# Inverting triangular blocks by a substitution of 32x32 instead of 16x16 blocks on GpSimd, without one level of small matmuls, and with unread products in the lead-in

## The chip, the cores and the metric

One core of a Trainium2 chip runs the whole layer in one launch. The time is the device's own, in microseconds, and the median of several executions counts. The engines are named as in the profile: PE is TensorE (products), PEld its weight loads, DVE is VectorE, ACT is ScalarE, POOL is GpSimd, and SP is SyncE, which only issues DMA transfers here.

## What is computed

The reference is a hybrid decoder layer in float32 for 512 tokens with 16 meta tokens ahead of them, width 1024, 16 heads of 64 channels. After a first layer norm one wide product (`w_in`) makes the inputs of two branches: attention in a sliding window of 128 tokens, and a recurrent mixer (RWKV-7). Both are gated per channel and added, projected (`w_out`), normalised with the residual, and sent through an MLP with a squared ReLU (1024 to 4096 to 1024) and a last norm. The mixer is where the change lies. For each head it keeps a 64x64 state S:

```
def step(S, inp):
    r_t, w_t, k_t, v_t, kk_t, a_t = inp
    sa = jnp.einsum('bhij,bhj->bhi', S, -kk_t)
    S = S * w_t[:, :, None, :] + sa[..., None] * (kk_t * a_t)[:, :, None, :] + v_t[..., None] * k_t[:, :, None, :]
    return S, jnp.einsum('bhij,bhj->bhi', S, r_t)
```

Taken in chunks of 64 tokens, the dependence of each step on the earlier ones within its chunk is a unit triangular system of 64x64 per chunk and head, N, and the kernel needs the inverse of that triangle.

## The kernel before

**Precision and the dense stream.** A float32 product of a weight tile with activations is made as three products of high and low parts: high by high, low by high, high by low (`three`, L476 to L478). ScalarE casts the high part of a weight tile (`whi`, L628), VectorE subtracts to get the low part (`wlo`, L630). These dense products run through the whole first two thirds of the kernel, since `w_in` has 52 tiles of 512 KB, and the mixer's and the attention's own products are woven between them. The MLP's products come at the end (L1560 to L1562 and L476 to L478 with `dps`).

**What sets the order.** Every operation is recorded by `op(engine, cost, fn, r=..., w=..., new=...)` with what it reads and writes. `ORDER`, a list of 2804 numbers written into the file, then says in which order the recorded operations are issued, and `SLOTS` which buffer of a ring each new tile gets. Each engine works through its own operations strictly in that order, and an operation waits for semaphores when what it reads or overwrites isn't done. So an operation that stands too early on an engine holds up all behind it.

**The lead-in.** x comes in four blocks of 128 tokens. Per block VectorE makes the statistics (L732, L735 to L737), GpSimd the power -0.5 (L740), and then ScalarE normalises blocks 0 and 1 (L752), VectorE blocks 2 and 3 (L755). TensorE transposes 16 tiles of blocks 0 and 1, the meta tokens' eight small ones (L764), and 16 tiles of blocks 2 and 3 (L787); the evictions (L797 on VectorE, L793 on ScalarE) put a scale and a bias on and split them into `hhi` and `hlo` (L802). Ahead of it TensorE transposes a table of per-channel rows (L710), which comes by DMA. Then the dense products begin.

**One pair of heads in the mixer.** Heads are taken two at a time (`rwkv`, pairs j = 0 to 7), with 8 chunks of 64 tokens. In `NT` lie the negated triangles N transposed, two heads above each other on 128 partitions. Per pair:

- the scores (L1000, 16 products of 128x128) give N and the matrices `GR`; VectorE masks them into `NT` (L1008) and `GR`;
- SyncE writes N to a scratch in DRAM (`Nd`, L1023 and L1025), and reads it back (L1077) so that each of the 64 diagonal 16x16 blocks, and two of the meta tokens, lies on one of 66 partitions of `Nf`;
- GpSimd inverts all 66 blocks at once by substitution. Step s multiplies the columns found so far with row s of N (L1092) and adds that on (L1096), 15 steps of two instructions;
- SyncE writes the result to DRAM (`Xd`, L1099; `Xrd`, L1100) and reads it back as the block diagonal of `XB` (L1103) and as `X1` (L1101);
- TensorE joins the 16x16 inverses to 32x32: 32 products X·N (L1118, `inv1`), a copy by ScalarE (L1137), 32 products (L1124, `inv2`), four copies (L1143). The records count two passes for a float32 product, so the profile shows 64 each;
- VectorE transposes the upper 32x32 blocks (L1146), and TensorE joins to 64x64: 16 products (L1129, `inv3`), copies (L1148), 16 products (L1134, `inv4`), copies into `XB` (L1150);
- the inverse is folded into the chunk matrices (`fold_w` L1160, `fold_g` L1173), the meta tokens take three small steps (`meta1` L1196, `meta2` L1200, `meta3` L1204), and the chain over the chunks follows (`links` L1234, outputs L1244).

GpSimd has other work in between: a power for the head norms (L1258), a sum for attention (L1297), an addition (L1268) and small copies (L903). The attention's scores are L1288.

The joins by 16, with X1, X2 and U in buffers of their own:

```
def inv1():
    for c in range(NCH):
        for g in range(4):
            r0, c0 = 32 * g, 32 * (g % 2)
            pe.matmul(w1()[r0 : r0 + 32, c, :], NT.t[r0 : r0 + B, c, c0 : c0 + 32], X1.t[r0 : r0 + B, c, :], start=True, stop=True)
```

The functions in full:

Of the kernel before, what the change touches and what calls it, by code (L numbers as in the profile page):

```python
# [20 lines left out]
P = 128  # L21
# [7 lines left out]
HD = 64  # L29
# [4 lines left out]
NBUCKETS = 32  # L34
LN_EPS = 1e-5
# [34 lines left out]
for _name, _c in ROWS:  # L70
# [167 lines left out]
def _constants():  # L238
# [10 lines left out]
    scan = np.ones(T)  # L249
    scan[0] = 0.0  # L250
    scan[NMETA::C] = 0.0
    out["scan"] = np.tile(scan, (P, 1))
# [19 lines left out]
    return np.ascontiguousarray(np.concatenate(cols, 1))  # L272


CONST = _constants()


class Ring:
# [80 lines left out]
def hybrid_layer_kernel(ctx: ExitStack, tc: tile.TileContext, I: dict, out: bass.AP):  # L359
# [221 lines left out]
    def setup():  # L581
        for t in rXB.slots:
            pool.memset(t, 0.0)
        for r in (rSVm, rBKm, rAXm):
            for t in r.slots:
                pool.memset(t, 0.0)
# [1110 lines left out]
```

## Time and profile before

| | |
|---|---|
| median of 3 executions | 929.36 us (928.54 to 929.58) |
| profiled execution, own time | 935.88 us |
| its span in the trace | 934.10 us |
| TensorE busy | 909.7 us, 7336 instructions |
| VectorE / ScalarE / GpSimd busy | 585.3 / 459.2 / 143.1 us |
| substitution on GpSimd (L1092 and L1096), busy | 42.4 + 41.6 us in 240 instructions |

The profiled execution is one run of its own, with its own time; durations are read from it and set against that time. A row of the timeline has start, length, engine, line, operation, output and inputs, and in brackets the engine's idle time before it with what ended it. In a row of grouped instructions stand the count, the busy sum and the mean in ns. `PEclk` or the granted clock is the share of the full TensorE clock that the chip's throttle allowed. TensorE's rows overlap, since products are pipelined; what one costs is read from the start of one to the start of the next.

### The profile page before, as it was taken

The page shows a single profiled execution, that of the slowest core. Times are in us where ns is not written, and L with a number is a line of the kernel's source. Part 1 is how long each engine was busy: PE and PEld are TensorE (multiplying, and loading weights), DVE is VectorE, ACT ScalarE, POOL GpSimd, SP SyncE. Part 2 cuts the span into 40 slices and gives each one's busy share as a digit, 9 for nine tenths or more (in the row PEclk, how much of TensorE's full clock was granted, in tenths as well). Part 3 has the DMA queues.
Part 4 walks back from the last instruction along what each step waited for, and adds up shares of the span by engine and source line. Part 5 has one row for each costly group of instructions (what it writes and reads, how often), then busy time and mean ns, then how long its engine had stood idle before and what let it go on. Part 6 is the DMA issues. An engine that isn't in the chain of part 4 may idle for free.

```text
span 934.1 us, 18420 instructions
## 1 busy us (share of the span) xinstructions
PE 909.7 (97%) x7336; PEld 788.4 (84%) x7336; DVE 585.3 (63%) x1154; ACT 459.2 (49%) x1109; POOL 143.1 (15%) x374
## 2 busy tenths in 40 slices
PE   4999999999999999999999999999999999999996
PEld 3999988989899889888998788888888888888885
DVE  7684766867768667777687779675423245443427
ACT  5756658468366573674757435643321133342120
POOL 2023041060330500603206002000000000000001
PEclk9999999999999988999999999999999999999999
DMA  6444123333343231333325521434223323332322
GB/s 232 142 130 106 48 71 95 103 80 98 70 108 95 69 99 38 99 88 72 101 69 162 145 91 46 159 113 135 91 91 103 100 91 97 107 91 90 100 82 90
DMA packets 85069, 93.22 MB, mean 100 GB/s; under 512 B 55142, under 2 KB 62056, under 8 KB 84984
## 3 DMA queue, kind: packets, MB, share of 16 engines
q1 hardware_dynamic: 84144, 90.88, 33.7%
q8 instruction: 57, 0.93, 0.4%
q10 hardware_dynamic: 840, 1.17, 0.3%
q14 instruction: 28, 0.23, 0.1%
HBM read 84.08 MB, written 9.00 MB: 100 GB/s over the span
## 4 chain that ended last, share of the span: by engine, by line
PE 93%; DVE 3%; ACT 1%; POOL 1%; DMA 1%; issue 1%; SPq 0%; DVEq 0%; ACTq 0%
PE g L476 12%; PE g L477 11%; PE g L478 11%; PE acc L1561 6%; PE acc L1560 6%; PE acc L1562 6%; PE dps L477 6%; PE dps L476 6%; PE dps L478 6%; PE g L1160 2%; PE g L1357 2%; PE g L1173 2%; PE g L1288 2%; PE g L1000 2%; PE g L1409 1%; PE g L1234 1%
## 5 line engine op out<-in xcount | busy, mean ns | idle before, releaser
L476 PE MATMUL g<-hhi,whi 128*128 128x512 f32 (+3 forms) x640 | 214.8, 336 | 0.0
L477 PE MATMUL g<-hlo,whi 128*128 128x512 f32 (+3 forms) x640 | 204.4, 319 | 0.0
L478 PE MATMUL g<-hhi,wlo 128*128 128x512 f32 (+3 forms) x640 | 204.1, 319 | 0.0
L456 DVE TENSOR_TENSOR wlo<-wraw,whi 128x512 fp32r<-128x512 f32 x118 | 76.4, 689 | 139.8 <-ACT whi L453 139.8
L453 ACT CAST whi<-wraw 128x512 fp32r<-128x512 f32 x118 | 67.5, 619 | 193.2 <-PE acc L1562 105.6
L476 PEld LDWEIGHTS g<-hhi,whi 128*128 128x128 f32 x640 | 121.7, 190 | 10.8 <-ACT res L901 1.0
L478 PEld LDWEIGHTS g<-hhi,wlo 128*128 128x128 f32 x640 | 121.6, 190 | 8.3
L477 PEld LDWEIGHTS g<-hlo,whi 128*128 128x128 f32 x640 | 121.7, 190 | 6.7
L630 DVE TENSOR_TENSOR wlo<-wraw,whi 128x512 fp32r<-128x512 f32 x126 | 86.6, 693 | 46.0 <-ACT whi L628 45.4
L628 ACT CAST whi<-wraw 128x512 fp32r<-128x512 f32 x126 | 76.7, 617 | 36.5 <-PE g L477 18.3
L1560 PE MATMUL acc<-whi,fhi 128*128 128x512 f32 x240 | 93.5, 389 | 0.0
L1562 PE MATMUL acc<-whi,flo 128*128 128x512 f32 x240 | 93.5, 389 | 0.0
L1561 PE MATMUL acc<-wlo,fhi 128*128 128x512 f32 x240 | 93.4, 389 | 0.0
L476 PE MATMUL dps<-h1hi,whi 128*128 128x512 f32 x232 | 90.4, 389 | 0.0
L477 PE MATMUL dps<-h1lo,whi 128*128 128x512 f32 x232 | 90.3, 389 | 0.0
L478 PE MATMUL dps<-h1hi,wlo 128*128 128x512 f32 x232 | 90.3, 389 | 0.0
L1092 POOL TENSOR_TENSOR ftmp<-Xf,Nf 66x15 f32<-66x15 f32 (+7 forms) x120 | 42.4, 354 | 125.0 <-DMA Nf<-Nd 117.1
L443 POOL TENSOR_TENSOR rsf<-rsf,mhalf 128x1 f32<-128x1 f32 x4 | 3.7, 934 | 344.3 <-DVE rsf L442 344.3
L1219 ACT ACTIVATE Z<-g,PC 64x64 f32<-64x64 f32 x64 | 19.8, 309 | 72.1 <-DVE Z L1216 32.8
L1560 PEld LDWEIGHTS acc<-whi,fhi 128*128 128x128 f32 x240 | 45.1, 188 | 9.4
L1562 PEld LDWEIGHTS acc<-whi,flo 128*128 128x128 f32 x240 | 45.1, 188 | 9.3
L1561 PEld LDWEIGHTS acc<-wlo,fhi 128*128 128x128 f32 x240 | 45.1, 188 | 9.3
(351 smaller groups left out, 1703.1 us busy)
## 6 DMA issues: line engine op xcount, KB each, us to landing
wraw<-in_w_ff_dram SPq DMA_DIRECT2D x64, 512.0 KB
wraw<-in_w_in_dram SPq DMA_DIRECT2D x52, 512.0 KB
wraw<-in_w_out_dram SPq DMA_DIRECT2D x14, 256.0 KB
res<-in_x_dram SPq DMA_DIRECT2D x4, 512.0 KB
Nd<-NT SPq DMA_DIRECT2D x16, 128.0 KB
G<-in_consts_dram SPq DMA_DIRECT2D x16, 128.0 KB
XB<-xtd SPq DMA_DIRECT2D x16, 128.0 KB
res<-in_x_dram SPq DMA_DIRECT2D x8, 256.0 KB
```

The lines of the kernel that those rows point to most:

```text
L453: act.copy(hi[:n, qs], raw[:n, qs])
L456: dve.tensor_tensor(lo[:n, qs], raw[:n, qs], hi[:n, qs].bitcast(F32), op=ALU.subtract)
L476: pe.matmul(ps, whi, xhi, start=first, stop=False)
L477: pe.matmul(ps, whi, xlo, start=False, stop=False)
L478: pe.matmul(ps, wlo, xhi, start=False, stop=last)
L628: AC(512, lambda hi=hi, qs=qs: act.copy(hi.t, raw.t[:, qs]), plain=True, r=[raw], w=[hi], new=[hi])
L630: f = lambda hi=hi, lo=lo, qs=qs, e=e: e.tensor_tensor(lo.t, raw.t[:, qs], hi.t.bitcast(F32), op=ALU.subtract)
L1092: sub(nj * nt, lambda s=s, nj=nj, nt=nt, tv=tv: se.tensor_tensor(tv(), Xf.t[:, 0:nj, s : s + 1].to_broadcast([NB, nj, nt]), Nf.t[:, s : s ...
L1219: op("ACT", 335, lambda: act.activation(Z.t[H2[1], c, 1, :], src(1), AF.Copy, scale=PC.t[H2[1], last : last + 1]), r=[ps, PC], w=[(Z, ("s" ...
L1560: pe.matmul(acc[b], xhi[:, k, bs], hi[:, ws], start=first, stop=False)
L1561: pe.matmul(acc[b], xhi[:, k, bs], lo[:, ws], start=False, stop=False)
L1562: pe.matmul(acc[b], xlo[:, k, bs], hi[:, ws], start=False, stop=last)
```

## The change

- GpSimd inverts 32x32 blocks (`BLK = 32`): 32 diagonal blocks and two of the meta tokens, 34, each spread over three partitions (`SPREAD = 3`, 102 in all) that hold 11 rows of the inverse each (rows g, g + 3, ...). There are 31 steps of two instructions. N is read into `Nf` three times, once for each third, the start matrix comes by DMA from a table of constants instead of two memsets, and the result is written in three transfers.
- `inv1`, `inv2`, the copies between them, `X1`, `Xrd` and the copy `Xr` go. The join to 64x64 (`inv3`, `inv4`) stays.
- `NT` and `GR` get two buffers each, `U` one; `WT` goes, and `fold_w`'s result overwrites `AT`.
- `meta1` reads 16 of 48 rows, and the scan of the decays is cut in two instructions, since its table of constants is half as long.
- Part of the constants goes into a buffer used later for something else (`tail`).
- `WARM = (9, 6)`: 9 products of 128x128 in the lead-in ahead of the first transposes and 6 between the two groups of 16, whose output nobody reads.
- `ORDER` and `SLOTS` are new.

```
+WARM = (9, 6)
+BLK = 32
+SPREAD = 3
+NROW = 11
+ZW = 560
+NBLK = 2 * (SEQ // C) * (C // BLK) + 2
...
 ORDER = [
-    0, 1, 6, 2, 3, 94, 5, 96, 45, 9, 44, 4, 7, 327, 8, 474, 11, 14, 19, 208, 10, 18, 782, 46,
...
-    rNT = ring("NT", rw, [P, NCH, C], 1)
-    rGR = ring("GR", rw, [P, NCH, P], 1)
+    rNT = ring("NT", rw, [P, NCH, C], 2)
+    rGR = ring("GR", rw, [P, NCH, P], 2)
...
-    rWT = ring("WT", rw, [P, NCH, P], 1)
...
-    rNf = ring("Nf", rw, [66, 16, 16], 1)
-    rXf = ring("Xf", rw, [66, 16, 16], 1)
-    rXr = ring("Xr", rw, [64, 16, 16], 1)
-    rtmp = ring("ftmp", rw, [66, 64], 2)
-    rX1 = ring("X1", rw, [P, NCH, 16], 1)
-    rX2 = ring("X2", rw, [P, NCH, 32], 1)
-    rU = ring("U", rw, [P, NCH, 32], 2)
+    rNf = ring("Nf", rw, [SPREAD * NBLK, BLK, BLK], 1)
+    rXf = ring("Xf", rw, [SPREAD * NBLK, NROW, BLK], 1)
+    rtmp = ring("ftmp", rw, [SPREAD * NBLK, 96], 1)
+    rU = ring("U", rw, [P, NCH, 32], 1)
...
+        wb, bw = Buf(rg), Buf(single(None))
+
+        def busy(key, n, cost, first, **k):
+            for i in range(n):
+                op("PE", cost, lambda: pe.matmul(wb.t[:, 0:P], ident, ident, start=True, stop=True), w=[wb, (bw, key)],
+                   new=[wb] if first and i == 0 else [], **k)
+
+        busy(0, WARM[0], 427, True, r=[bident])
...
+                if h == 1 and i == 0:
+                    busy(1, WARM[1], 260, False, r=[(bw, 0), (bw, "h")])
...
-        for s in range(B - 1):
-            nj, nt = s + 1, B - 1 - s
-            tv = lambda nj=nj, nt=nt: tmps[0].t[:, 0 : nj * nt].rearrange("p (j t) -> p j t", j=nj)
-            sub(nj * nt, lambda s=s, nj=nj, nt=nt, tv=tv: se.tensor_tensor(
+        for s in range(BLK - 1):
+            nj, nt = s // SPREAD + 1, BLK - 1 - s
+            tv = lambda nj=nj, nt=nt: tmp.t[:, 0 : nj * nt].rearrange("p (j t) -> p j t", j=nj)
+            sub(nj * nt, lambda s=s, nj=nj, nt=nt, tv=tv: pool.tensor_tensor(
                 tv(), Xf.t[:, 0:nj, s : s + 1].to_broadcast([NB, nj, nt]),
                 Nf.t[:, s : s + 1, s + 1 :].to_broadcast([NB, nj, nt]), op=ALU.mult),
...
-        op("SP", 330, lambda: nc.sync.dma_start(blocks(Xd.t, 0, [BSTEP, NB], [C, B], [1, B]), Xf.t), wire=1000, r=[Xf], w=[Xd], new=[Xd])
-        op("SP", 500, lambda: nc.sync.dma_start(Xrd.t, Xr.t), wire=100, r=[Xr], w=[Xrd], new=[Xrd])
-        op("SP", 460, lambda: nc.sync.dma_start(X1.t, blocks(Xrd.t, 0, [B, P], [8 * B * B, NCH], [1, B])), wire=2300, r=[Xrd], w=[X1], new=[X1])
+        for g in range(SPREAD):
+            nr = len(range(g, BLK, SPREAD))
+            op("SP", 330, lambda g=g, nr=nr: nc.sync.dma_start(
+                blocks(Xd.t, g * C, [BSTEP, NBLK], [SPREAD * C, nr], [1, BLK]), Xf.t[g * NBLK : (g + 1) * NBLK, 0:nr]),
+               wire=500, r=[Xf], w=[(Xd, g)], new=[Xd] if g == 0 else [])
...
-        op("PE", 480, inv1, r=[NT, X1, XB], w=[up], new=[up, U, U2, X2], mode="Q")
-        AC(128, more=-58, fn=lambda: act.copy(U.t[:, :, 0:B], w1()), plain=True, r=[up], w=[U])
-        op("PE", 446, inv2, r=[U, XB], w=[up], mode="Q")
...
-        op("DVE", 850, lambda: [dve.transpose(X2.t[lo_[e]], XB.t[lo_[e], :, lo_[e]]) for e in range(2)], r=[XB], w=[X2])
-        op("PE", 432, inv3, r=[NT, X2], w=[up], mode="Q")
+        op("DVE", 850, lambda: [dve.transpose(U2.t[lo_[e]], XB.t[lo_[e], :, lo_[e]]) for e in range(2)], r=[XB], w=[(U2, 0)], new=[U2])
+        op("PE", 432, inv3, r=[NT, (U2, 0), XB], w=[up], new=[up], mode="Q")
...
-                pe.matmul(ms.t[m16, e * HD : (e + 1) * HD], AKm.t[:, e, :], SVm.t[:, e, :], start=True, stop=True)
+                pe.matmul(ms.t[m16, e * HD : (e + 1) * HD], AKm.t[32:48, e, :], SVm.t[32:48, e, :], start=True, stop=True)
```

In the changed kernel the lines have other numbers: the dense products are L496 to L498, the unread ones L721, the transposes L813, the scores L1034, the substitution L1122 and L1126, the load of `Nf` L1113, the writes of the result L1130, the load of `XB` L1134, `inv3` L1146, `inv4` L1151, `meta1` L1202, `meta2` L1206.

On TensorE, this is the end of pair 0's inversion before, where the two levels of joins stand apart among dense products (`khi` is the attention's keys, `U` and `X` are the joins' operands):

```order
L1118 MATMUL g<-X_181,NT_157 32x16 x32
L1288 MATMUL g<-khi_214,e_131 128x256 x4
L1124 MATMUL g<-XB_175,U_183 16x16 x32
L476 MATMUL g<-hhi,whi 128x264
```

```order
L1129 MATMUL g<-X_182,NT_157 32x32 x16
L1196 MATMUL g<-SVm_159,AKm_161 16x64 x2
L1288 MATMUL g<-khi_214,e_131 128x256 x4
L1134 MATMUL g<-XB_175,U_184 32x32 x16
L1200 MATMUL g<-RHm_167,XTm_169 16x64 x2
L476 MATMUL g<-hhi,whi 128x512
```

The same place in the changed kernel; L1034, with `G` and `BK`, are pair 1's scores, in two halves:

```order
L1294 MATMUL g<-khi_208,res_125 128x256 x4
L1034 MATMUL g<-G_143,BK_139 128x128 x8
L1146 MATMUL g<-U_180,NT_157 32x32 x16
L1202 MATMUL g<-SVm_161,AKm_163 16x64 x2
L1034 MATMUL g<-G_143,BK_139 128x128 x8
L1151 MATMUL g<-XB_176,U_180 32x32 x16
L1206 MATMUL g<-RHm_169,XTm_171 16x64 x2
L496 MATMUL g<-hhi,whi 128x264
```

The first level has left TensorE's row, and the next pair's scores, which stood behind `fold_g` before, now stand ahead of and between this pair's last two joins.

On VectorE in the lead-in, before, `res_128` and `res_127` are the last two blocks of x:

```order
L732 BN_STATS stx_236<-res_128 128x6 x2
L735 BN_AGGR mvx_237<-stx_236 128x2
L736 TENSOR_SCALAR rsx_238<-mvx_237 128x1
L737 TENSOR_SCALAR nmx_239<-mvx_237 128x1
L797 TENSOR_SCALAR e_129<-g,vc 128x256 x2
L797 TENSOR_SCALAR e_134<-g,vc 128x256 x2
L630 TENSOR_TENSOR wlo<-wraw,whi 128x512
L802 TENSOR_TENSOR hlo<-e_129,hhi 128x2x256
L732 BN_STATS stx_232<-res_127 128x6 x2
```

And in the changed kernel, where L758 are the statistics, L781 the normalising, and L798 and L799 belong to the meta tokens:

```order
L758 BN_STATS stx_230<-res_128 128x6 x2
L798 TENSOR_TENSOR bias_186<-g,vc 128x128
L761 BN_AGGR mvx_231<-stx_230 128x2
L762 TENSOR_SCALAR rsx_232<-mvx_231 128x1
L763 TENSOR_SCALAR nmx_233<-mvx_231 128x1
L799 TENSOR_TENSOR bias_186<-bias_186,vc 128x128
L758 BN_STATS stx_226<-res_127 128x6 x2
L781 TENSOR_SCALAR res_128<-res_128,mvx_231,rsx_232 128x512
```

The statistics of the last block have moved ahead of the evictions of the first 16 transposes and of the first weight split.

On TensorE, the changed lead-in starts with unread products (L721) around the rows' transpose (L736) and the meta tokens' (L790):

```order
L721 MATMUL g<-con 128x128 x3
L736 MATMUL g<-con,zwa 128x114
L721 MATMUL g<-con 128x128
L790 MATMUL g<-con,sb_187 128x16 x8
L721 MATMUL g<-con 128x128 x5
L813 MATMUL g<-con,res_125 128x128
```

Before, the rows' transpose came first, then the 16 transposes, and the meta tokens' eight behind those; six more unread products now stand between the two groups of 16.

More of the change, by code (lines that the diff above doesn't have):

```diff
@@ L248, in _constants @@
     out["mak"] = np.stack([tri & hi[:, None], tri & lo[:, None]], 1).reshape(P, -1)
-    scan = np.ones(T)
+    scan = np.ones(NMETA + SEQ // 2)
     scan[0] = 0.0
@@ L263, in _constants @@
     bucket = np.where(dist < 16, dist, np.minimum(large, NBUCKETS - 1))
+    out["bones"] = bones
     out["onehot"] = p[:, None] == bucket[None, :]
+    rowof = SPREAD * np.arange(NROW)[None, :, None] + (p // NBLK)[:, None, None]
+    out["start"] = (rowof == np.arange(BLK)[None, None, :]).reshape(P, -1)
     at = 0
@@ L381, in ahead @@
         tc.cur_priority += n
-    con = cst.tile([P, CONST.shape[1]], F32, name="con")
+    con = cst.tile([P, KEPT], F32, name="con")
     def cv(name):
@@ L472, in hybrid_layer_kernel @@
     hlo = hpool.tile([P, KT, T], F32R, name="hlo")
-    xtd = [dr.tile([P * 544], F32, name=f"xtd{i}") for i in range(3)]
+    xtd = [dr.tile([P * ZW], F32, name=f"xtd{i}") for i in range(3)]
     def three(ps, whi, wlo, xhi, xlo, first=True, last=True):
@@ L583, in setup @@
             pool.memset(t, 0.0)
-        for r in (rSVm, rBKm, rAXm):
+        for r in (rSVm, rBKm, rAXm, rNBm):
             for t in r.slots:
@@ L840, in head @@
         tb, tbs = Buf(rg), Buf(rbias)
-        op("PE", 323, lambda: pe.matmul(tb.t[0:HEADS, 0:P], relb, cv("onehot")[0:NBUCKETS], start=True, stop=True), r=[bcon, brelb], w=[tb], new=[tb], mode="H")
+        op("PE", 323, lambda: pe.matmul(tb.t[0:HEADS, 0:P], relb, tail.t[0:NBUCKETS, 1], start=True, stop=True), r=[tail, brelb], w=[tb], new=[tb], mode="H")
         AC(P, lambda: act.copy(tbs.t[0:HEADS, 0, :], tb.t[0:HEADS, 0:P]), plain=True, r=[tb], w=[tbs], new=[tbs])
@@ L909, in rwkv, with sums @@
         Ls = Buf(re_)
-        op("DVE", 1170, lambda: dve.tensor_tensor_scan(Ls.t, cv("scan"), tw.t, 0.0, op0=ALU.mult, op1=ALU.add), r=[tw], w=[Ls], new=[Ls])
+        def sums():
+            w = NMETA + SEQ // 2
+            dve.tensor_tensor_scan(Ls.t[:, 0:w], cv("scan"), tw.t[:, 0:w], 0.0, op0=ALU.mult, op1=ALU.add)
+            dve.tensor_tensor_scan(Ls.t[:, w:], cv("scan")[:, NMETA:], tw.t[:, w:], 0.0, op0=ALU.mult, op1=ALU.add)
+        op("DVE", 1240, sums, r=[tw], w=[Ls], new=[Ls])
         Px, Pm, PC, iP = Buf(rPx), Buf(rPm), new("PC", rPC), Buf(re_)
@@ L1083, in rwkv @@
[L1083 to L1092 removed]
+        Nf, Xf, XB, XTm = Buf(rNf), Buf(rXf), Buf(rXB), Buf(rXTm)
@@ new lines, in rwkv @@
+        Xd, tmp = Buf(rXd), Buf(rtmp)
+        NB = SPREAD * NBLK
+        at_ = CONSTS["start"][0]
+        op("SP", 330, lambda: nc.sync.dma_start(Xf.t.rearrange("p i t -> p (i t)"), I["consts"][0:NB, at_ : at_ + NROW * BLK]), wire=500, w=[Xf], new=[Xf])
+        for g in range(SPREAD):
+            op("SP", 330, lambda g=g: nc.sync.dma_start(Nf.t[g * NBLK : (g + 1) * NBLK], blocks(Nd.t, 0, [BSTEP, NBLK], [C, BLK], [1, BLK])),
+               wire=1200, r=[Nd], w=[(Nf, g)], new=[Nf] if g == 0 else [])
@@ L1101, in rwkv @@
-        op("SP", 460, lambda: nc.sync.dma_start(X1.t, blocks(Xrd.t, 0, [B, P], [8 * B * B, NCH], [1, B])), wire=2300, r=[Xrd], w=[X1], new=[X1])
+               port=1, r=[Nf, Xf], w=[tmp], new=[tmp] if s == 0 else [])
+            sub(nj * nt, lambda s=s, nj=nj, tv=tv: pool.tensor_tensor(
+                Xf.t[:, 0:nj, s + 1 :], Xf.t[:, 0:nj, s + 1 :], tv(), op=ALU.add), r=[tmp], w=[Xf])
+        for g in range(SPREAD):
+            nr = len(range(g, BLK, SPREAD))
+            op("SP", 330, lambda g=g, nr=nr: nc.sync.dma_start(
+                blocks(Xd.t, g * C, [BSTEP, NBLK], [SPREAD * C, nr], [1, BLK]), Xf.t[g * NBLK : (g + 1) * NBLK, 0:nr]),
+               wire=500, r=[Xf], w=[(Xd, g)], new=[Xd] if g == 0 else [])
@@ L1172, in fold_g @@
                     for e in range(2):
-                        pe.matmul(gq[e].t[:, c * P : (c + 1) * P], WT.t[H2[e], 4 * i + c, :], GR.t[H2[e], 4 * i + c, :], start=True, stop=True)
-            op("PE", 892, fold_g, r=[(WT, i), GR], w=gq, new=gq, mode="H")
+                        pe.matmul(gq[e].t[:, c * P : (c + 1) * P], AT.t[H2[e], 4 * i + c, :], GR.t[H2[e], 4 * i + c, :], start=True, stop=True)
+            op("PE", 892, fold_g, r=[(AT, i), GR], w=gq, new=gq, mode="H")
             for e in range(2):
@@ L1450, in hybrid_layer_kernel @@
     bh1 = Buf(single(None))
[L1451 removed]
+    gone = (rNT, rGR, rAT, rXB, rNf, rXf, rtmp, rU, rBK, rPx)
     def swap():
```

86 lines of the change are left out of this document (28 added, 58 removed), and 307 rows, old and new, of tables (ORDER, SLOTS).

## The prediction

> **What bounds the kernel now.** I read the page's totals first, then the chain that ended last, then what TensorE waited for, then busy time by stretch, and single rows where the change works.
>
> ```profile
> span 934.1 us, 18420 instructions
> PE 909.7 (97%) x7336; PEld 788.4 (84%) x7336; DVE 585.3 (63%) x1154; ACT 459.2 (49%) x1109; POOL 143.1 (15%) x374
> ```
>
> ```profile
> PE 93%; DVE 3%; ACT 1%; POOL 1%; DMA 1%; issue 1%; SPq 0%; DVEq 0%; ACTq 0%
> ```
>
> TensorE is busy 97% of the span and carries 93% of the chain; GpSimd, which gets the new work, is busy 15%. All that TensorE waited for:
>
> ```profile
> PE g L710 <- DMA zwa<-in_rows_dram: 5.6, 1, 5.6
> PE g L787 <- ACT res L752: 4.7, 2, 3.3
> PE g L787 <- DVE res L755: 3.0, 1, 3.0
> PE g L1357 <- DVE pown L1350: 1.0, 1, 1.0
> PE g L477 <- DVE h1lo L1504: 0.8, 1, 0.8
> PE g L1196 <- ACT SVm L1191: 0.8, 1, 0.8
> PE g L1490 <- DVE res L1484: 0.6, 1, 0.6
> ```
>
> The columns are total, times and longest. The first three, 13.3 us, lie in the lead-in; the other four sum to 3.2 us over the remaining 900. Between them TensorE never stands still. So a product removed behind the lead-in should shorten the run by its own length, as long as what stands behind it in TensorE's order is ready that much earlier. Time off another engine is worth nothing there.
>
> The same for a stretch of 100 us in the time mix: the stretch and its length, busy time of TensorE, its weight loads, VectorE, ScalarE and GpSimd, then the granted TensorE clock (1.00), the DMA share and GB/s:
>
> ```profile
> 200.00:300.00 100.00, 100.00 (x1172) 90.12 (x1171) 72.51 (x156) 64.23 (x177) 20.73 (x56) 1.00 0.34 91
> ```
>
> **Removed products.** Around the first pair's inversion TensorE shows this (start, length, operation):
>
> ```profile
> 92.69 0.73 PE L1118 MATMUL g<-X,NT 16*32 16x16 f32 x64
> 93.35 1.13 PE L1288 MATMUL g<-khi,e 64*128 64x256 f32 x8
> 94.41 0.68 PE L1124 MATMUL g<-XB,U 32*16 32x16 f32 x64
> 95.03 0.39 PE L476 MATMUL g<-hhi,whi 128*128 128x264 f32 x1
> 95.26 0.29 PE L477 MATMUL g<-hlo,whi 128*128 128x264 f32 x1
> 95.38 0.29 PE L478 MATMUL g<-hhi,wlo 128*128 128x264 f32 x1
> ```
>
> Lengths overlap, so I count from start to start. The first group goes (L1118): 93.35 − 92.69 = 0.66 us. The second (L1124): 95.03 − 94.41 = 0.62. Per pair 1.28, for eight pairs **−10.2 us**. No row has them beside other TensorE work, and the products behind them have no wait of their own in the list above, so all of it lies on the path.
>
> Each group also breaks the stream. The first wide product behind it takes 95.26 − 95.03 = 0.23 to the next start, the second 0.12. Of the two breaks in a pair I let one go, since L1288 between them remains: 8 × 0.11 = **−0.9 us**; at most both, −1.8; at least nothing.
>
> The first product of the meta tokens now reads 16 rows instead of 48. In the rows above the depth of a product doesn't matter: L1118 contracts over 16 rows and L1124 over 32, and the same count takes 0.66 and 0.62 us. So I cost that at nothing. ScalarE's and VectorE's dropped copies, the scan cut in two and the halved ring of buffers cost nothing here: ScalarE was at 49% and VectorE at 63%, and neither appears among TensorE's waits in this stage but for the 0.8 us at L1196.
>
> **The substitution, and what hides it.** GpSimd gets 62 instructions a pair instead of 30, over 1991 instead of 680 elements a partition for each of multiply and add. In pair 2:
>
> ```profile
> 188.17 0.21 POOL L1092 TENSOR_TENSOR ftmp<-Xf,Nf 66x15 f32<-66x15 f32 x1 [18.98 <-DMA Nf<-Nd]
> 188.46 0.22 POOL L1096 TENSOR_TENSOR Xf<-Xf,ftmp 66x15 f32<-66x15 f32 x1
> 192.57 0.31 POOL L1092 TENSOR_TENSOR ftmp<-Xf,Nf 66x63 f32<-66x63 f32 x1
> 192.96 0.86 POOL L1096 TENSOR_TENSOR Xf<-Xf,ftmp 66x63 f32<-66x63 f32 x1
> ```
>
> Start to start it is 0.29 us for 15 elements (188.17 to 188.46) and 0.39 for 63 (192.57 to 192.96): about 0.26 us + 2.1 ns an element. So 30 instructions take 7.8 + 2 × 680 × 0.0021 = 10.7 us undisturbed, 62 take 16.1 + 2 × 1991 × 0.0021 = 24.5; 102 partitions instead of 66 I count at nothing, since they work side by side. The write of this pair's result is issued at 201.13 (row below), so the chain took 12.9 instead of 10.7, a factor 1.21, from other GpSimd work between and from stretched instructions such as the 0.86. I take 24.5 × 1.21 = 29.6.
>
> The stage ends when the inverse is back for the product L1129. TensorE's rows on the chain and SyncE's issues for the same pair:
>
> ```profile
> 165.01 0.62 PE g L1129 x32
> 177.42 1.78 PE g L1000 x32
> 222.20 0.62 PE g L1129 x32
> ```
>
> ```profile
> 201.13 0.31 SPq L1099 DMA_DIRECT2D xtd<-Xf  x1
> 205.07 2.33 SPq L1103 DMA_DIRECT2D XB<-xtd  x2
> ```
>
> From the scores (L1000, 177.42) to the first substitution instruction (188.17) it was 10.8 us; from the result's write (201.13) through the round trip over DRAM to the end of the XB issue (207.40) 6.3, and I add 2 for landing and the transposes. Before, the inversion had from 177.42 to 222.20, 44.8 us. In the new order the scores of the next pair stand around this pair's last two product groups (L1146 and L1151 of the changed kernel, which are L1129 and L1134 here), with double NT and GR buffers to allow it, so a pair has from one L1129 to the next: 222.20 − 165.01 = 57.2, less the 1.4 that the pair saves, 55.8. Needed are 10.8 + 29.6 + 8.3 = 48.7, so about 7 us are left, and I cost the longer substitution at **nothing**. SyncE's two extra loads of Nf and two extra writes of Xf (0.3 us each as issues, by the rows above) eat about 1 of that; what is queued behind the write that waits for GpSimd are weight loads, which are ahead of use by several buffers.
>
> If that cover fails, each us over 55.8 is a us of TensorE standing at L1146. A sign of danger is that GpSimd and VectorE meet: the same 63 elements took 0.31 and 0.86 us. A two-input instruction of VectorE, in the MLP with GpSimd idle and in this stage:
>
> ```profile
> L456 DVE TENSOR_TENSOR wlo<-wraw,whi 128x512 fp32r<-128x512 f32 x118 | 76.4, 689 | 139.8 <-ACT whi L453 139.8
> L630 DVE TENSOR_TENSOR wlo<-wraw,whi 128x512 fp32r<-128x512 f32 x126 | 86.6, 693 | 46.0 <-ACT whi L628 45.4
> ```
>
> 689 against 693 ns: VectorE isn't slowed, so GpSimd alone would pay, and in the pair shown it pays within the factor 1.21. The Trainium skill ("GPSIMD Engine Reference", § 8 Key points) speaks against the change here: GpSimd shares its SBUF interfaces with VectorE, with contention for VectorE instructions in a 2-port mode or with two SBUF inputs. That GpSimd's rows stretch agrees; that VectorE's own don't shows who pays. By that rule a chain twice as long meets twice as much of VectorE's work, which is what the slower rival below needs.
>
> **The lead-in.** TensorE, then VectorE:
>
> ```profile
> 18.89 3.57 PE L787 MATMUL g<-con,res 128*128 128x128 f32 x16 [3.00 <-DVE res L755]
> 22.22 0.37 PE L476 MATMUL g<-hhi,whi 128*128 128x264 f32 x1
> ```
>
> ```profile
> 12.21 1.90 DVE L797 TENSOR_SCALAR e<-g,vc 128x256 f32<-128x256 f32 x4 [0.60 <-PE g L787]
> 15.23 1.28 DVE L732 BATCH_NORM_STATS2 stx<-res 128x6 f32<-128x512 f32 x2
> 22.50 1.00 DVE L797 TENSOR_SCALAR e<-g,vc 128x256 f32<-128x256 f32 x2 [0.80 <-PE g L787]
> ```
>
> The last quarter's statistics (15.23) stood behind 3.0 us of evictions and splits (12.21 to 15.23); now they stand ahead, so its normalised rows, waited for until 18.89, are ready near 16. But VectorE's displaced 3.0 us must still be done before dense products have operands, and VectorE idled only 0.60 + 0.80 = 1.4 us between 12 and 23. The second gain is the clock. Of TensorE alone:
>
> ```profile
> 18.81:22.23 3.42, 3.34 (x17) 0.50 0.17 14
> 22.23:25.64 3.41, 3.41 (x30) 1.00 0.45 159
> 169.00:172.41 3.41, 3.41 (x15) 0.50 0.51 193
> 343.08:356.73 13.65, 13.65 (x126) 0.50 0.25 78
> ```
>
> The second 16 transposes ran at half clock (0.50), for one window of 3.4 us right behind the wait of 3.00: 16 in 3.33 us (18.89 to 22.22). At full clock they would take half, 1.7 us less. The 15 unread products fill such waits: nine before the first transposes, six before the second 16. At the cold pitch of 0.21 us they last 1.9 and 1.3 us. The nine lie in TensorE's 9 us of waiting; the six can push the transposes by up to 1. So the bounds are −3.1 (1.7 + 1.4) and +1; I take **−2.0**, nearer the gain, because both mechanisms have their row.
>
> Against that gain the Trainium skill ("TensorE: Matmul & The Clock Gate", Part 4) says that transposes don't engage the full clock. Here the trace disagrees: the window 18.81 to 22.23 held 16 transposes and one product, and the next, with the first dense products, was granted the full clock (1.00).
>
> **New waits.** Scores, L1146 and L1151 stand closer together than their counterparts did. Such a place cost 0.8 us at L1196 before, and could even go (−0.8); eight pairs at half that would be +3.2. I take an eighth of a us a pair, **+1.0**, as nearly all such places in the list cost nothing.
>
> **Sum.** −10.2 − 0.9 − 2.0 + 1.0 = −12.1 us. The profiled execution took 935.88 us with its span of 934.10, while the runs had a median of 929.36; the difference is mostly the half clock above, (3.41 + 13.65) / 2 = 8.5 us lost behind stretches of small products. On the same conditions it would be 923.8; against the median, with as many such drops as before, **917.3 us**. What a measurement of this kernel can tell from no change is about 0.2%, 1.9 us.
>
> **The rivals.**
> - *Only the products count*: the lead-in ends at VectorE, breaks and waits cancel. 929.4 − 10.2 = 919.2. For it: VectorE's 1.4 us of idle time. 0.20.
> - *Transposes do not count as work for the clock*: then the dense stream starts with one 3.4 us window at half clock, 1.7 us lost, 919.0. Against it: the dense starts above. 0.04. This is the rule of the Trainium skill cited under the lead-in.
> - *One more stretch at half clock* such as that of 13.65 us falls into most runs: + 6.8, 924.1. The drops follow small products, and the order is new; but fewer small products are left. 0.07.
> - *TensorE's time isn't shortened*: what is removed turns into waits for DMA or VectorE in place, 929. Against it: 100.00 us busy out of 100 with DMA at 0.34. 0.04.
> - *Slower: the substitution outgrows the pair.* GpSimd's last pair was stretched far more:
>
> ```profile
> 493.25 0.48 POOL L1092 TENSOR_TENSOR ftmp<-Xf,Nf 66x15 f32<-66x15 f32 x1 [13.92 <-DMA Nf<-Nd]
> 514.09 0.56 POOL L1096 TENSOR_TENSOR Xf<-Xf,ftmp 66x15 f32<-66x15 f32 x1
> ```
>
> That is 21.4 us, twice 10.7. If the factor 2.0 holds for the longer chain, it takes 49.0, the pair needs 10.8 + 49.0 + 8.3 = 68.1 against 55.8, and TensorE stands 12.3 us. It decides from a factor of (55.8 − 19.1) / 24.5 = 1.5, and one such pair eats the whole gain; three give 917.3 + 36.9 = 954. Against it: much of those 21.4 us is a fixed load (a normaliser's power, a pad, a sum), which doesn't grow with the chain: 24.5 + 10.7 = 35.2, needing 54.3, still within. 0.06.
>
> **How the numbers follow.** The forecast gets the remaining 0.59. Low end: all terms at their good ends, −10.2 − 1.8 − 3.1 − 0.8 = −15.9, 913.5, less one 3.4 us window at half clock that the median may lose (1.7): 911.8. High end: −10.2 + 1.0 + 3.2 = −6.0, 923.4, and the case of the longer half-clock stretch, 924.1. Outside lie same and slower, 0.10, and some tails. Faster by over 0.2% is every case but those two: 0.90; same 0.04; slower 0.06.
>
> **What would show it.** Right: L1118 and L1124 are gone and TensorE's busy time outside the lead-in falls by 10 to 11 us; no TensorE wait at L1146 over 1 us; GpSimd's chain takes 25 to 35 us a pair; the second 16 transposes take about 1.7 us and the first dense product starts before 21 us. Wrong: rows of TensorE waiting at L1146 for DMA into XB or for VectorE's transposes, of several us a pair; dense products of the lead-in waiting for VectorE for 3 us or more; or half-clock stretches longer than 17 us in sum.

## The result: slower, and the profile after

| | before | after |
|---|---|---|
| median | 929.47 us (928.54 to 930.81, 6 runs) | 1016.33 us (1014.70 to 1020.61, 6 runs) |
| ratio | | 1.094, interval 1.092 to 1.096 |
| profiled execution, own time / span | 935.88 / 934.10 us | 1016.97 / 1015.2 us |
| mean granted TensorE clock | 0.987 | 0.963 |

The forecast was 917.3, with a range of 911.8 to 924.1. The totals in the page of the changed kernel:

```profile
span 1015.2 us, 16641 instructions
PE 933.0 (92%) x6342; PEld 799.4 (79%) x6342; DVE 589.0 (58%) x1154; ACT 450.2 (44%) x1069; POOL 240.9 (24%) x616
```

TensorE has 994 records fewer (1024 of the removed products, less 30 of the unread ones), and yet is busy 23 us longer and stands 82 us instead of 24. What it waited for, longest first (total, times, longest):

```profile
PE g L1240 <- ACT Z L1225: 13.0, 3, 7.3
PE g L1146 <- DVE U L1153: 12.9, 8, 4.5
PE g L1270 <- DVE sm L1330: 6.3, 1, 6.3
PE g L1363 <- ACT pall L1355: 4.7, 1, 4.7
PE g L924 <- DVE e L689: 3.7, 1, 3.7
PE g L1240 <- DVE Z L1222: 3.6, 2, 2.9
```

The whole list sums to 74 us, 68 of them behind the lead-in, where it had been 3.2. Only 12.9 stand at L1146, the product that needs the inverse, where the prediction had put its slower rival. The largest is in the chain over the chunks (L1240), which waits for ScalarE, and the rest is spread.

The other part is the clock. A row of busy times by stretch, with the granted clock third from the end:

```profile
220.00:250.00 30.00, 23.72 (x145) 21.58 (x144) 14.08 (x25) 18.06 (x52) 25.54 (x59) 0.89 0.27 76
```

Of 30 us TensorE stood 6, and the clock was 0.89. Over the span, 0.963 against 0.987 is (0.037 × 1015 − 0.013 × 934) = 25 us more lost to half clock than before. That is an upper bound, as a part of the half clock fell on the waits themselves: from 144.3 on the granted clock was 0.50, and TensorE stood until 148.8. So the long waits cost twice: once as they last, and again behind them.

**Where the waits come from.** One place, followed back. SyncE's issues in pair 1, then ScalarE, TensorE and GpSimd in the same 50 us:

```profile
123.56 0.26 SPq L1113 DMA_DIRECT2D Nf<-Nd  x1
123.87 5.28 SPq L1111 DMA_DIRECT2D Xf<-in_consts_dram  x1
129.24 0.66 SPq L1281 DMA_DIRECT2D tbd<-tbh  x1
129.95 9.00 SPq L1113 DMA_DIRECT2D Nf<-Nd  x2
139.00 5.53 SPq L639 DMA_DIRECT2D wraw<-in_w_in_dram  x2
```

```profile
147.33 0.62 ACT L644 CAST whi<-wraw 128x512 fp32r<-128x512 f32 x1 [7.75 <-DMA wraw<-in_w_in_dram]
...
148.47 0.31 ACT L1225 ACTIVATE Z<-g,PC 64x64 f32<-64x64 f32 x1
```

```profile
148.84 0.80 PE L1240 MATMUL g<-Z,G 128*128 128x128 f32 x2 [7.34 <-ACT Z L1225]
149.29 0.57 PE L496 MATMUL g<-hhi,whi 128*128 128x264 f32 x1
149.65 0.42 PE L497 MATMUL g<-hlo,whi 128*128 128x264 f32 x1
149.87 0.42 PE L498 MATMUL g<-hhi,wlo 128*128 128x264 f32 x1
```

```profile
145.55 0.24 POOL L1122 TENSOR_TENSOR ftmp<-Xf,Nf 102x31 f32<-102x31 f32 x1 [41.00 <-DMA Nf<-Nd]
...
173.45 0.22 POOL L1126 TENSOR_TENSOR Xf<-Xf,ftmp 102x11 f32<-102x11 f32 x1
```

Read it from below. GpSimd's chain itself lasts 173.67 − 145.55 = 28.1 us, as forecast (29.6). But it begins 22 us after the first load of `Nf` was issued (123.56), where before it was 2.3 (pair 2); in the other seven pairs of the changed kernel it is 16.8 to 17.9. And the issues themselves take long: 9.00 us for two loads, and the issue of the load of constants between them 5.28 us. The weights behind them (`wraw`) leave SyncE at 139.00 to 144.53 and are there at 147.33, when ScalarE, which works in its own order, has stood 7.75 us for them. Its next piece of `Z`, a small thing that has nothing to do with weights, comes at 148.47, and TensorE's link, which needs it, has stood 7.34. The dense products behind start 0.22 us apart instead of 0.12: half clock. In all, ScalarE waited for weights of `w_in` this long (total, times, longest); before, no such wait is listed:

```profile
ACT whi L644 <- DMA wraw<-in_w_in_dram: 39.2, 11, 7.7
```

How slow the load is, over all pairs (issue time in ns: least, median, most), in the changed kernel and then in the kernel before:

```profile
L1113 SPq DMA_DIRECT2D Nf<-Nd x24: 242/5057/7170, 56.4 to 558.8; - x24
```

```profile
L1077 SPq DMA_DIRECT2D Nf<-Nd x8: 306/318/452, 62.9 to 490.4; - x8
```

These are 1088 and 1056 packets: 34 blocks of 32 rows, and 66 of 16. While little but such loads runs, the busy share of the 16 DMA engines (the last three columns are clock, share and GB/s) is this, after and before:

```profile
204.00:214.00 10.00, 10.00 (x95) 9.15 (x95) 5.55 (x13) 5.43 (x13) 0.00 (x0) 1.00 0.18 28
```

```profile
186.78:187.70 0.92, 0.92 (x5) 0.75 (x4) 0.92 (x2) 0.47 (x1) 0.00 (x0) 1.00 0.79 74
```

0.18 of 16 is 2.9 engines at most, 0.79 is 12.6. The trace doesn't number the engines, but 34 is 2 × 17 and 66 is 6 × 11. The guess for the experiments (**theory A**): a transfer's packets go to as many engines as divide the outer count of its pattern, up to 16, which is 2 for 34 and 11 for 66. The Trainium skill ("DMA: Bandwidth & Descriptors", section "Why a DMA increments its semaphore by 16 and not by 1") has this rule: the number of engines is the largest up to 16 that divides the slowest dimension of both sides. The runs with 36 and 38 blocks below agree with it (0.92 and 5.65 us an issue). The prediction had not weighed it.

### The profile page after: what moved, and what is told of

The parts are those of the page before. It is cut to its first block, busy times and chain, and to the rows that moved or that the text cites. A ratio compares the mean times of both kernels' runs of the same rounds, so it can differ in the third digit from the quotient of the medians.

```text
span 1015.2 us, 16641 instructions
## 1 busy us (share of the span) xinstructions
PE 933.0 (92%) x6342; PEld 799.4 (79%) x6342; DVE 589.0 (58%) x1154; ACT 450.2 (44%) x1069; POOL 240.9 (24%) x616
## 5 line engine op out<-in xcount | busy, mean ns | idle before, releaser
L496 PE MATMUL g<-hhi,whi 128*128 128x512 f32 (+3 forms) x640 | 219.1, 342 | 3.3 <-DVE res L689 1.8
L498 PE MATMUL g<-hhi,wlo 128*128 128x512 f32 (+3 forms) x640 | 208.8, 326 | 1.9 <-DVE wlo L646 1.8
L497 PE MATMUL g<-hlo,whi 128*128 128x512 f32 (+3 forms) x640 | 208.7, 326 | 0.8 <-DVE hlo L830 0.8
L496 PEld LDWEIGHTS g<-hhi,whi 128*128 128x128 f32 x640 | 126.1, 197 | 17.4 <-issue 4.4
L498 PEld LDWEIGHTS g<-hhi,wlo 128*128 128x128 f32 x640 | 125.7, 196 | 11.4 <-DVE wlo L646 3.0
L497 PEld LDWEIGHTS g<-hlo,whi 128*128 128x128 f32 x640 | 126.1, 197 | 8.4 <-DVE hlo L830 1.0
L1122 POOL TENSOR_TENSOR ftmp<-Xf,Nf 102x84 f32<-102x84 f32 (+23 forms) x248 | 89.4, 361 | 178.1 <-DMA Nf<-Nd 154.0
L646 DVE TENSOR_TENSOR wlo<-wraw,whi 128x512 fp32r<-128x512 f32 x126 | 87.9, 707 | 49.4 <-ACT whi L644 48.7
L1126 POOL TENSOR_TENSOR Xf<-Xf,ftmp 102x84 f32<-102x84 f32 (+23 forms) x248 | 95.6, 385 | 18.8
L496 PE MATMUL dps<-h1hi,whi 128*128 128x512 f32 x232 | 90.3, 389 | 0.0
L498 PE MATMUL dps<-h1hi,wlo 128*128 128x512 f32 x232 | 90.2, 389 | 0.0
```

What stands on the lines that cost most here:

```text
L496: pe.matmul(ps, whi, xhi, start=first, stop=False)
L497: pe.matmul(ps, whi, xlo, start=False, stop=False)
L498: pe.matmul(ps, wlo, xhi, start=False, stop=last)
L646: f = lambda hi=hi, lo=lo, qs=qs, e=e: e.tensor_tensor(lo.t, raw.t[:, qs], hi.t.bitcast(F32), op=ALU.subtract)
L1122: sub(nj * nt, lambda s=s, nj=nj, nt=nt, tv=tv: pool.tensor_tensor(tv(), Xf.t[:, 0:nj, s : s + 1].to_broadcast([NB, nj, nt]), Nf.t[:, s : ...
L1126: sub(nj * nt, lambda s=s, nj=nj, tv=tv: pool.tensor_tensor(Xf.t[:, 0:nj, s + 1 :], Xf.t[:, 0:nj, s + 1 :], tv(), op=ALU.add), r=[tmp], w= ...
```

## The experiments

**Cutting the transfers.** First the loads and the writes of the changed kernel, 34 blocks, cut into 32 and 2:

```
-            op("SP", 330, lambda g=g: nc.sync.dma_start(Nf.t[g * NBLK : (g + 1) * NBLK], blocks(Nd.t, 0, [BSTEP, NBLK], [C, BLK], [1, BLK])),
+            op("SP", 330, lambda g=g: [nc.sync.dma_start(Nf.t[g * NBLK + a : g * NBLK + b], blocks(Nd.t, a * BSTEP, [BSTEP, b - a], [C, BLK], [1, BLK]))
+                                       for a, b in ((0, NBLK - 2), (NBLK - 2, NBLK))],
...
-                blocks(Xd.t, g * C, [BSTEP, NBLK], [SPREAD * C, nr], [1, BLK]), Xf.t[g * NBLK : (g + 1) * NBLK, 0:nr]),
+                blocks(Xd.t, a * BSTEP + g * C, [BSTEP, b - a], [SPREAD * C, nr], [1, BLK]), Xf.t[g * NBLK + a : g * NBLK + b, 0:nr])
+                for a, b in ((0, NBLK - 2), (NBLK - 2, NBLK))],
```

Expected, on record before the run:

> The changed kernel with each of the three loads of Nf and each of the three writes of the result cut into one of 32 blocks and one of the two meta blocks. Theory A: a transfer's packets go to as many DMA engines as divide the outer count of its pattern, so 34 blocks (2 x 17) run on two engines, 32 on sixteen. Then the time from the first load of Nf to the first substitution instruction falls from 17.5 us (pair 2 of the changed kernel) to 4 to 6, from the write of the result to the issue of XB from 7.6 to 4 to 5, the chain of a pair from 67 to about 51 us, and the whole from 1016 to 915 to 935 us. Theory B: three copies in packets of 128 B are simply too much for the queue (3264 packets a pair instead of 1056): more issues change nothing, the load stays over 14 us and the time over 1005. Theory C, that of my slower rival (GpSimd's chain is what outgrows the pair): the load gets shorter, but the time stays over 990.

Measured: 931.67 us against 930.78 for the kernel before on the same chip, ratio 1.001 (0.999 to 1.003). So 85 of the 87 us lost go with this edit alone; theories B and C fall. Its totals and its longest waits:

```profile
span 930.1 us, 16704 instructions
PE 904.3 (97%) x6342; PEld 778.1 (84%) x6342; DVE 589.9 (63%) x1154; ACT 450.0 (48%) x1069; POOL 249.2 (27%) x616
```

```profile
PE g L721 <- DMA con<-in_consts_dram: 3.1, 1, 3.1
PE g L1417 <- ACT Z L1101: 2.2, 1, 2.2
PE g L1272 <- DVE res L1267: 1.8, 3, 1.1
```

GpSimd's first instruction of pair 1, whose first load is issued at 113.09:

```profile
113.09 0.80 SPq L1113 DMA_DIRECT2D Nf<-Nd  x2
```

```profile
122.25 0.24 POOL L1123 TENSOR_TENSOR ftmp<-Xf,Nf 102x31 f32<-102x31 f32 x1 [22.71 <-DMA Nf<-Nd]
```

9.2 us instead of 22, with other issues between; no wait is left at the product that needs the inverse. The mean granted clock is back at 0.995. Against the changed kernel, for the same 6342 records, TensorE stands 56 us less (25.8 instead of 82.2) and is busy 29 us less (904.3 instead of 933.0).

With only the loads cut (one execution, as in all runs below for which no ratio is given; the kernel before varied between 929 and 938 us on these chips):

> Only the three loads of Nf are cut into 32 and 2 blocks, the writes stay at 34. Theory A: 12 to 13 of the 16 us go, the chain of a pair is 54 us and the time 925 to 945. Theory B: over 1005. Theory C: over 990.

954.13 us, above what was expected: the writes, with a third as many packets as the loads, still cost 22 us.

**Another count.** Nothing is cut here, but the substitution gets 36 blocks, and then 38; those added hold zeros and are used by nobody:

```
-ZW = 560
-NBLK = 2 * (SEQ // C) * (C // BLK) + 2
+ZW = 592
+META0 = 2 * (SEQ // C) * (C // BLK)
+NBLK = 36
...
```

> 36 blocks instead of 34 for the substitution, the two added ones hold zeros and are not used; nothing is cut. 36 has the divisor 12. Theory A: twelve engines, the first load of Nf to the first substitution instruction takes 5 to 7 us, the time is within 10 us of the run with both cut. Theory B: 3456 packets, a little slower than the changed kernel, over 1010.

> 38 blocks (2 x 19), four unused. Theory A: again two engines, 12% more packets: the load takes 18 to 20 us instead of 17.5 and the time is 1015 to 1050. Theory B: the same within what can be told apart, 1015 to 1050. If padding itself did something, it would be as fast as 36.

932.24 and 1035.95 us. The issue of a load of `Nf` in each, 36 first:

```profile
L1116 SPq DMA_DIRECT2D Nf<-Nd x24: 308/920/2297, 57.5 to 478.1; - x24
```

```profile
L1116 SPq DMA_DIRECT2D Nf<-Nd x24: 242/5645/7357, 57.5 to 574.7; - x24
```

More packets at 36 than at 34, and five times faster; at 38 the median is 5645 against 5057 ns, 12% more for 12% more packets on as few engines. The count's divisors decide it (36 has 12, 38 has 2), not the number of packets, nor padding. 1088 packets in 5.06 us on two engines are 9.3 ns a packet and engine; 1216 in 5.65 us on two are 9.3 as well, and 1152 in 0.92 us on twelve 9.6.

**Which way the slow transfers cost.** Two ways are open: the inversion's own chain is late, or what stands behind the slow transfers is. Into the kernel with both cut go two more transfers of 34 blocks from `Nd` to a scratch nobody reads, behind a pair's loads, and in the next run two of 32:

```
+                nc.sync.dma_start(blocks(scr, 0, [BSTEP, 34], [C, BLK], [1, BLK]), blocks(Nd.t, 0, [BSTEP, 34], [C, BLK], [1, BLK])) for q in range(2 * (g == 2))],
...
```

> The kernel with both cut, and behind each pair's last load of Nf two more transfers of 34 blocks that copy Nd to a scratch buffer nobody reads: no wait of the inversion gets longer, but 2176 packets lie on the same queue ahead of the weights. Theory W: half of the loss of the changed kernel comes that way, weights and tables queued behind the slow transfers; then 945 to 975 us. Rival: only the longer chain of the pair counted; then 930 to 935.

> The same with the two added transfers of 32 blocks. Theory A says sixteen engines: the 2048 packets are through in 2 to 3 us, 930 to 936 us. If the number of packets is what loads the queue, as slow as with 34.

988.37 with 34, 938.83 with 32: the two engines cost 50 us. The 7 us of the bytes and packets lie within what the kernel before varies. In pairs 1, 5 and 7, though, the order issued the third load ahead of another one, so these chains were late too. So the same with the two transfers behind the last load in every pair:

> As the run with two added transfers of 34 blocks, but here they stand behind the last load of Nf in every pair; in the first such run they stood ahead of one of the loads in pairs 1, 5 and 7, whose load to substitution took 19 to 24 us instead of 6 to 9, so that these chains were late as well. In that run the five other pairs lost about 24 us together, 4.8 each. Theory W, weights late behind slow transfers with the inversion's own chain on time: 8 x 4.8 = 38 us on top of 932, 955 to 980 us. Rival: the loss of the first run came from its three late chains; then under 945.

981.08 us (ratio 1.055, 1.050 to 1.061). SyncE's issues of pair 1, and then what ScalarE and TensorE waited for:

```profile
121.16 5.16 SPq L1115 DMA_DIRECT2D Nf<-Nd  x4
126.36 8.74 SPq L1117 DMA_DIRECT2D scr<-Nd  x2
135.21 6.10 SPq L641 DMA_DIRECT2D wraw<-in_w_in_dram  x2
```

```profile
ACT whi L646 <- DMA wraw<-in_w_in_dram: 52.3, 10, 11.8
```

```profile
PE g L1246 <- ACT Z L1231: 21.3, 4, 11.4
```

The loads are all out ahead of the two, and still about 49 us are lost: weights behind the slow transfers, ScalarE behind the weights, TensorE's links behind ScalarE. That is just over the expected range (955 to 980); I had taken 4.8 us a pair and it is 6. The inversion's chain wasn't on time everywhere even so: the load took as long as with both cut (9.1 and 9.2 us to the first substitution instruction in pair 1), but in pairs 1, 4 and 7 the substitution lasted 41 to 42 us instead of 28 to 35, in pair 1 because GpSimd stood 13.45 us for ScalarE's `whi`. So late weights make the chain late as well.

The other way, the chain late and no slow transfer: 34 multiplications more on GpSimd at the start of each substitution.

```
+            sub(..., lambda ...: [pool.tensor_tensor(
+                tmp.t[:, 0:96].rearrange("p (j t) -> p j t", j=3), Nf.t[:, 0:3, :], Nf.t[:, 0:3, :], op=ALU.mult) for q in range(34 * (s == 0))] and 0 or pool.tensor_tensor(
```

> The kernel with both cut, and 34 multiplications of 96 elements more on GpSimd ahead of each pair's substitution, whose result is overwritten: about 15.6 us a pair, so that a pair's chain is as long as in the changed kernel (67 us), while no slow transfer lies on the queue. Theory W (most of the loss comes from weights queued behind the slow transfers): 940 to 970 us. Rival, the mechanism of my slower case (the chain outgrows the pair): 985 to 1015, with TensorE waiting at inv3.

1042.31 us: 111 us more than with both cut, so this way alone can cost as much. The rival's price was real, but not at the place it named. VectorE's waits:

```profile
DVE sm L1312 <- POOL sb L1306: 45.1, 5, 13.9
...
DVE res L1268 <- POOL rs L1267: 30.2, 4, 15.5
```

```profile
PE g L1273 <- DVE res L1268: 24.7, 3, 15.0
```

GpSimd's small jobs, the attention's pad and the head norms' power, stand in its order behind the longer substitution, VectorE waits for them, and TensorE for VectorE. The run is not a clean copy of the loss, since GpSimd is busy there where in the changed kernel it stands; both hold up what is behind. In the changed kernel both ways act at once, and their shares in the 85 us can't be added up from these runs.

**The kernel before, with its transfers on two engines.** 62 (2 × 31) and 4 blocks instead of 66, in the load shown and in the write of the result likewise:

```
-lambda: nc.sync.dma_start(Nf.t, blocks(Nd.t, 0, [BSTEP, NB], [C, B], [1, B]))
+lambda: [nc.sync.dma_start(Nf.t[a:b], blocks(Nd.t, a * BSTEP, [BSTEP, b - a], [C, B], [1, B])) for a, b in ((0, 62), (62, 66))]
...
```

> The kernel before the change, with the load of Nf and the write of the result cut into 62 (2 x 31) and 4 blocks instead of 66 at once (6 x 11). Theory A says two engines instead of eleven for the 62: from the issue of the load to the first substitution instruction 6 to 8 us instead of 2.3, and by theory W 934 to 960 us. Rival: with 64-byte packets or so few of them nothing changes, 929 to 932.

953.89 us, with 933.71 for the kernel before beside it, one run each. In pair 2:

```profile
189.57 3.92 SPq L1077 DMA_DIRECT2D Nf<-Nd  x2
```

```profile
194.84 0.21 POOL L1092 TENSOR_TENSOR ftmp<-Xf,Nf 66x15 f32<-66x15 f32 x1 [21.88 <-DMA Nf<-Nd]
```

5.3 us to the first substitution instead of 2.3, less than the 6 to 8 expected, and 20 us in all: an awkward outer count costs time without any part of the change. ScalarE's waits for weights of `w_in` (10.0 us in all, none listed before) are there too.

**Another queue for the loads.** The changed kernel, its three loads issued by GpSimd:

```
-            op("SP", 330, lambda g=g: nc.sync.dma_start(Nf.t[g * NBLK
+            op("SP", 330, lambda g=g: nc.gpsimd.dma_start(Nf.t[g * NBLK
...
```

> The changed kernel as it is, with 34 blocks, but GpSimd issues the three loads of Nf on its own queue instead of SyncE. If what waits behind them waits because it is in the same queue, the weights get by and it takes 950 to 990 us. If the two engines themselves are what is full, weights wait there too: over 1000.

1182.26 us, far worse than either expectation, and it doesn't answer the question:

```profile
146.58 3.08 POOL L1113 DMA_DIRECT2D Nf<-Nd  x1 [20.12 <-DMA Nd<-NT]
159.46 3.05 POOL L1113 DMA_DIRECT2D Nf<-Nd  x1 [9.79 <-issue]
173.20 3.05 POOL L1113 DMA_DIRECT2D Nf<-Nd  x1 [10.68 <-issue]
185.51 0.23 POOL L1122 TENSOR_TENSOR ftmp<-Xf,Nf 102x31 f32<-102x31 f32 x1 [9.27 <-DMA Nf<-Nd]
```

Each load issued from GpSimd takes it 3.05 us and 10 more before the next, so the chain begins 39 us after the first. Whether the weights would get by on a queue of their own stays open.

**What is missing between 931.7 and 917.** Two runs on the kernel with both cut. In the first the substitution stops after 16 of 31 steps, so the inverse is incomplete; in the second the unread products of the lead-in are 2 columns wide instead of 128:

```
-            sub(nj * nt, lambda s=s, nj=nj, nt=nt, tv=tv: pool.tensor_tensor(
+            sub(nj * nt, lambda s=s, nj=nj, nt=nt, tv=tv: s < 16 and pool.tensor_tensor(
```

```
-                op("PE", cost, lambda: pe.matmul(wb.t[:, 0:P], ident, ident, start=True, stop=True), ...
+                op("PE", cost, lambda: pe.matmul(wb.t[:, 0:2], ident, ident[:, 0:2], start=True, stop=True), ...
```

> The kernel with loads and writes cut into 32 and 2 blocks, but the substitution stops after 16 of 31 steps: the inverse is left incomplete, so the output is another. GpSimd's chain should take about 13 us undisturbed instead of 24.5, as long as before the change. Theory R1: the longer chain on GpSimd, by its length or by slowing VectorE, still costs what is missing between 931.7 us and my 917; then the time falls to 916 to 922. Theory R2: what is missing is many short waits of TensorE in the new order, elsewhere than at the inversion; then it stays at 929 to 932.

> The kernel with both cut, but the 15 unread products are 2 columns wide instead of 128, so that they take next to no time. Theory: they keep the clock up; without them the second 16 transposes run at half clock, the first dense product starts 1 to 2 us later and the time is 932.5 to 934. Rival: VectorE bounds the lead-in anyway, the time stays within 0.5 us of 931.7.

The short substitution: 925.52 us, ratio to before 0.994 (0.992 to 0.996), between the two expectations. The longer chain costs 6 us even with fast transfers, as far as this run shortens it: in six of the eight pairs the result's write still left 5 to 12 us after the last step. Without the unread products' width: 931.98, ratio to before 1.0015 (0.9998 to 1.0033), no difference to 931.67. The last unread products, the second 16 transposes and the first dense product, and then those of the changed kernel:

```profile
15.16 1.40 PE L721 MATMUL g<-con 128*128 128x2 f32 x12
16.42 1.94 PE L813 MATMUL g<-con,res 128*128 128x128 f32 x16
18.12 0.37 PE L496 MATMUL g<-hhi,whi 128*128 128x264 f32 x1
```

```profile
14.78 1.50 PE L721 MATMUL g<-con 128*128 128x128 f32 x12
16.12 1.91 PE L813 MATMUL g<-con,res 128*128 128x128 f32 x16
17.78 0.37 PE L496 MATMUL g<-hhi,whi 128*128 128x264 f32 x1
```

1.70 and 1.66 us from the first of the 16 to the dense products: full clock in both. But the run doesn't take the unread work away, as its expectation assumed: the products of 2 columns hold TensorE 1.26 us (15.16 to 16.42), those of 128 columns 1.34. It shows that their width does nothing; whether the lead-in needs them at all is not shown.

## Why the prediction was wrong, point by point

- **What bounds the kernel**: TensorE, right. It is also why each late piece shows in full.
- **The removed products**: they are gone, and their price was right, but not that all of it lies on the path. Counted from start to start from 30 us on, without waits and half clock, L1118 and L1124 took 5.3 and 4.9 us in the profiled execution before, yet all products together 884 us before and 879 with both cut. About half of the 10.2 us comes back as longer distances between other products, some 1.5 us each at the scores and the chain over the chunks. That and the new waits below are why the best whole version only ties with the kernel before.
- **The substitution's length**: right. 29.6 us was forecast; 28.1 in pair 1, 28.1 to 33.8 over all pairs. VectorE's two-input split of the weights took 707 ns (L646) instead of 693, so GpSimd still pays nearly alone.
- **The step that failed**: "From the scores (L1000, 177.42) to the first substitution instruction (188.17) it was 10.8 us" was carried over unchanged into the sum of 48.7, and "SyncE's two extra loads of Nf and two extra writes of Xf (0.3 us each as issues, by the rows above) eat about 1". I priced a transfer by its issue of before. In the changed kernel the loads alone take 22 us from issue to use in pair 1 and about 17 in the others, because each runs on few engines, and 0.3 us became 5.06. The row that I had, 2.3 us for a pattern of 66 × 16, was no row for one of 34 × 32: the outer count decides. The sum of 48.7 measured 67.7 in pair 2, by these rows (scores, first substitution instruction, last issue of `XB`):

```profile
192.54 2.06 PE L1034 MATMUL g<-G,BK 64*128 64x128 f32 x32
217.39 0.24 POOL L1122 TENSOR_TENSOR ftmp<-Xf,Nf 102x31 f32<-102x31 f32 x1 [23.67 <-DMA Nf<-Nd]
257.70 0.58 SPq L1134 DMA_DIRECT2D XB<-xtd  x1
```

24.85 us instead of 10.8 to the first substitution instruction, 30.88 instead of 29.6 from there to the write (248.27), and from the write to the end of the `XB` issue 10.01 instead of 6.3, with the same 2 for landing. That is 11.9 over the 55.8 that a pair had.

- **What stands behind them**: "weight loads, which are ahead of use by several buffers" was the second half of the same failure. In pair 1 SyncE spent 123.87 to 139.00 on slow issues ahead of them, 15 us, and ScalarE stood 7.75 us (row above): that is more than the buffers cover. Two slow transfers a pair with nobody waiting for them cost 49 us.
- **The slower rival** had the right outcome and a real mechanism (111 us for 15.6 us a pair), but its cause, GpSimd stretched, didn't happen, and its place was not L1146. The loads and writes took the pair past its 55.8 us instead, and TensorE stood at L1146 12.9 us in all, not 12 a pair. A chance of 0.06 was too small for a chain with 7 us to spare in which one of the terms had no row of its own.
- **The lead-in**: the size was about right. The dense products begin at 17.78 instead of 22.22, VectorE holds one of them 0.8 us later, and some hundred dense products on 2.1 us are left (34.81 instead of 36.89; 0.8 in the execution with both cut). The transposes took the forecast 1.7 us. Of the two reasons, the statistics moved ahead are seen: the 16 transposes come without the 3.00 us wait in front of them. What the unread products add isn't shown, since the run with narrow ones holds TensorE nearly as long.
- **The clock rule** of the Trainium skill on transposes ("TensorE: Matmul & The Clock Gate", Part 4) was weighed rightly: the prediction's row, full clock behind a window of 16 transposes, stands against it. The changed kernel adds no test of it: the second 16 transposes ran at 0.11 us each, but behind unread products (1.3 us of them in the two executions above).
- **New waits**, + 1.0: mis-sized. With both cut, waits behind the lead-in sum to 10.9 us instead of 3.2. 6 us go with GpSimd's length (short substitution). Of the remaining 8 us to the forecast, about 3 are waits (6.3 us in that run's list instead of 3.2, most of them under a microsecond) and most of the rest the longer distances between products named above; which part of the order makes them wasn't settled.

## What to carry to other kernels

Before a tile's shape is changed, look at the outer count of every transfer that carries it: 34 blocks ran on few engines and cost 85 us, 32 + 2, or 36 with two idle, did not. A transfer's price isn't its issue, and not only its own: all that is queued behind it, and on each engine that works in a fixed order all that stands behind the piece that came late, pays as well. Where a sum leaves 7 us of slack in 56, each of its terms needs a row of the same shape, or the slower case needs more than a few per cent.

## What the runs showed of the hardware

- While transfers of 34 × 32 packets of 128 B ran, the share of the 16 engines was 0.18; an issue took 5.06 us at the median, 9.3 ns a packet and engine if two engines carry it. For 36 × 32 it took a fifth of that, 0.92 us.
- SyncE's issue blocks when the transfers ahead are slow: 5.06 us at the median instead of 0.32, and the next issue of any kind with it (5.28 us for a table of constants, 5.06 for weights).
- The same load issued by GpSimd cost it 3.05 us and about 10 us until its next issue.
- Behind the lead-in of the changed kernel, all six waits of TensorE of over 3.5 us (3.74 to 7.34) were followed by products at half clock (0.22 instead of 0.12 us a step); of the seven of 2 to 3 us, three were. Over the span that is at most 25 us more than before.
- Twelve records of unread products held TensorE 1.26 us with 2 columns and 1.34 us with 128.
